# Moving the transposes of the left operand from the tensor engine to the vector engine in a matmul with layer norm

## Chip, cores, metric

One core of a Trainium2 chip. The metric is the device time of one execution in microseconds (us), median of several executions. All runs quoted are fast. A profiled execution has a span 1.8 to 2.1 us below the time measured for it.

## The reference

```python
def setup_inputs():
    m, k, n = 2048, 2048, 2048      # a, b, gamma, beta are fp32 normal draws; eps = 1e-5

def reference(a, b, gamma, beta, eps):
    x = np.matmul(a, b)
    mean = np.mean(x, axis=-1, keepdims=True)
    var = np.var(x, axis=-1, keepdims=True)
    normalized = (x - mean) / np.sqrt(var + eps)
    return (gamma * normalized + beta).astype(np.float32)
```

## The kernel before

All of `b` is loaded and cast to fp16 in SBUF. The rows of `a` are worked through in 16 blocks of 128 rows. The matmuls of this kernel take both operands with K on the partitions, but `a` is loaded with its rows there, so each block is transposed: 16 transposes of 128x128 on TensorE into PSUM, which ScalarE copies to SBUF. A block is then 64 matmuls (16 steps of K times 4 quarters of 512 columns). VectorE takes statistics from PSUM, ScalarE copies the product out of PSUM, and VectorE subtracts and scales in two steps a quarter. The first four blocks are done together, first their left half of the columns, then their right half, because `b` is still arriving.

```python
    a16p = ctx.enter_context(tc.tile_pool(name="a16p", bufs=4))
    # ... (cut)
    def emit_transposes_half(i, h):
        a16 = a16_lst[i]
        at = at_lst[i]
        t_ps = psum.tile([P, n_kt // 2, P], FP16, tag="tps", bufs=1,
                         name=f"tps{i}_{h}")
        for j in range(n_kt // 2):
            nc.tensor.transpose(t_ps[:, j, :], a16[:, ts(h * 8 + j, P)], ident)
        nc.scalar.copy(at[:, ds(h * 8, 8), :], t_ps)
    # ... (cut)
    def quarter_done(i, q):
        nc.vector.bn_stats(bnst_l[i][:, q, :], c_ps_l[i][q])
        x_sb = xpool.tile([P, NB], FP32, tag="x_sb", name=f"x_{i}_{q}")
        nc.scalar.copy(x_sb, c_ps_l[i][q])
    # ... (cut) the steady blocks:
            for kt in range(n_kt):
                for q in range(n_nb):
                    emit_mm(i, q, kt)
                if kt == 4 and i + 2 < n_mt:
                    alloc_at(i + 2)
                    emit_transposes_half(i + 2, 0)
                if kt == 9 and i + 2 < n_mt:
                    emit_transposes_half(i + 2, 1)
            for q in range(n_nb):
                quarter_done(i, q)
        emit_ln_stats(i)
        if i - n_start < n_start:
            emit_ln_stt(i - n_start)      # outputs of one of the first four blocks
        emit_ln_stt(i, split_out=(2 if not last else 4))
```

Of the kernel before, what the change touches and what calls it, by code (L numbers as in the profile page):

```python
# [16 lines left out]
def kernel(  # L17
# [12 lines left out]
    K2, N = b.shape  # L30
    assert K == K2
    assert M % P == 0 and K % P == 0 and N % 2048 == 0
# [5 lines left out]

    n_start = 4
    assert n_mt > n_start  # L40

    if isinstance(eps, bass.AP):
        eps_ap = eps
        eps_val = None
    else:
        eps_ap = None
        eps_val = float(eps)
# [4 lines left out]
    atp = ctx.enter_context(tc.tile_pool(name="atp", bufs=6))  # L52
    xpool = ctx.enter_context(tc.tile_pool(name="xpool", bufs=20))
    upool = ctx.enter_context(tc.tile_pool(name="upool", bufs=4))
    cpool = ctx.enter_context(tc.tile_pool(name="cpool", bufs=2))
    stat = ctx.enter_context(tc.tile_pool(name="stat", bufs=4))
# [5 lines left out]
    ident = konst.tile([P, P], FP16)  # L62

    b16 = bpool.tile([P, n_kt, N], FP16)

    def emit_a_load(i, split=1):
        a16 = a16p.tile([P, K], FP16, tag="a16", name=f"a16_{i}")
        w = K // split
        for s in range(split):
            nc.gpsimd.dma_start(a16[:, ds(s * w, w)], a[ts(i, P), ds(s * w, w)])  # L70
        return a16

    a16_lst = [None] * (n_mt + 2)
    at_lst = [None] * (n_mt + 1)

    def alloc_at(i):
        at_lst[i] = atp.tile([P, n_kt, P], FP16, tag="at", name=f"at{i}")

    def emit_transposes_half(i, h):
        a16 = a16_lst[i]  # L80
        at = at_lst[i]
        t_ps = psum.tile([P, n_kt // 2, P], FP16, tag="tps", bufs=1,
                         name=f"tps{i}_{h}")
        for j in range(n_kt // 2):
            nc.tensor.transpose(t_ps[:, j, :], a16[:, ts(h * 8 + j, P)], ident)  # L85
        nc.scalar.copy(at[:, ds(h * 8, 8), :], t_ps)  # L86

    def emit_transposes(i):
        alloc_at(i)
        emit_transposes_half(i, 0)  # L90
        emit_transposes_half(i, 1)
        return at_lst[i]

    bnst_l = [None] * n_mt
    c_ps_l = [[None] * n_nb for _ in range(n_mt)]
    x_sb_l = [[None] * n_nb for _ in range(n_mt)]
    rstd_l = [None] * n_mt
    mv_l = [None] * n_mt

    def alloc_q(i, q):  # L100
        if bnst_l[i] is None:
            bnst_l[i] = stat.tile([P, n_nb, 6], FP32, tag="bnst", name=f"bnst{i}")
        c_ps_l[i][q] = psum.tile([P, NB], FP32, tag="c_ps", bufs=7,
                                 name=f"cps_{i}_{q}")

    def emit_mm(i, q, kt):
        nc.tensor.matmul(  # L107
            c_ps_l[i][q],
            at_lst[i][:, kt, :],
            b16[:, kt, ds(q * NB, NB)],  # L110
            start=(kt == 0),
            stop=(kt == n_kt - 1),
        )

    def quarter_done(i, q):
        nc.vector.bn_stats(bnst_l[i][:, q, :], c_ps_l[i][q])  # L116
        x_sb = xpool.tile([P, NB], FP32, tag="x_sb", name=f"x_{i}_{q}")
        nc.scalar.copy(x_sb, c_ps_l[i][q])  # L118
        x_sb_l[i][q] = x_sb

    def emit_ln_stats(i):
        mv = stat.tile([P, 2], FP32, name=f"mv{i}")
        nc.vector.bn_aggr(mv, bnst_l[i])  # L123
        ve = stat.tile([P, 1], FP32, name=f"ve{i}")
        nc.vector.tensor_tensor(ve, mv[:, 1:2], eps_t, AluOp.add)  # L125
        sq = stat.tile([P, 1], FP32, name=f"sq{i}")
        nc.scalar.activation(sq, ve, ActFn.Sqrt)  # L127
        rstd = stat.tile([P, 1], FP32, name=f"rstd{i}")
        nc.vector.reciprocal(rstd, sq)  # L129
        mv_l[i] = mv  # L130
# [45 lines left out]
    for i in range(6, n_mt):  # L176
        a16_lst[i] = emit_a_load(i)
# [97 lines left out]
```

## Time and profile before

| | before |
|---|---|
| time, median of 15 runs | 268.2 us |
| TensorE: from first product matmul to last | 11.3 to 256.9 us |
| one steady block of 128 rows | 14.81 us, of it 13.8 matmuls and 0.9 transposes |
| VectorE busy in such a block | 13.6 us in the first four, 8.3 later |
| tail after the last matmul | 10.6 us |

The table is to be read from TensorE's side: it never waits between 29 us and the end, so the span is a start, then 13.8 + 0.9 us for each block, then a tail.

### The profile page before, as it was taken

Reading aid. Unit: us, or ns where it says so; the run is one execution under the profiler, and the core shown is the slowest. Engines: PE = TensorE matmul, PEld = TensorE weight load, DVE = VectorE, ACT = ScalarE, POOL = GpSimd, SP = SyncE. Lnnn points to the kernel's source line nnn. Section 1 sums busy time; section 2 is a strip of 40 time slices with the busy share of each in tenths; the row PEclk is TensorE's granted clock in tenths of the full one; section 3 lists DMA queues with packets and bytes.
Section 4 is the critical chain, followed back from the end, with each engine's and each line's share of the span. In section 5 each row is a group of like instructions: output and inputs, shape, how many; then the busy total and the mean of one; then the engine's idle time right before and its main releaser. Section 6 shows DMA issues by size and latency. Waiting matters only on the chain.

```text
span 267.5 us, 3149 instructions
## 1 busy us (share of the span) xinstructions
PE 242.8 (91%) x1280; PEld 117.0 (44%) x1280; DVE 131.9 (49%) x242; ACT 74.1 (28%) x114; POOL 30.3 (11%) x61
## 2 busy tenths in 40 slices
PE   1349999999999999999999999999999999999940
PEld 0125544454444445454444444454544444444410
DVE  0000000600059179898989183654729092847753
ACT  1314300750046133313315142323123151303110
POOL 8343433440000000000000000000000000000000
PEclk9999999999999999999999999999999999999995
DMA  5999999999930524937475515330211103030304
GB/s 74 164 209 210 210 213 208 210 210 370 214 70 0 176 59 161 219 160 156 175 152 211 159 29 167 71 157 0 117 42 80 78 29 130 0 157 2 157 0 157
DMA packets 12974, 35.85 MB, mean 134 GB/s; under 512 B 1440, under 2 KB 1952, under 8 KB 12704
## 3 DMA queue, kind: packets, MB, share of 16 engines
q0 software_dynamic: 8064, 18.88, 37.3%
q1 hardware_dynamic: 4896, 16.78, 15.7%
q8 instruction: 10, 0.16, 0.3%
q14 instruction: 4, 0.03, 0.0%
HBM read 35.65 MB, written 16.78 MB: 196 GB/s over the span
## 4 chain that ended last, share of the span: by engine, by line
PE 89%; DMA 4%; POOL 2%; DVE 2%; issue 0%; DVEq 0%; POOLq 0%
PE cps L107 84%; PE tps L85 5%; DMA b<-in_b_dram 4%; POOL a L70 2%; DVE u L140 1%; DVE c L144 1%; DVE bnst L116 0%; DVEq L270 0%; POOL b L164 0%; POOL b L153 0%; POOL ident L155 0%; DVE mv L123 0%; DVE ve L125 0%; DVE rstd L129 0%; POOLq L155 0%
## 5 line engine op out<-in xcount | busy, mean ns | idle before, releaser
L107 PE MATMUL cps<-b,at 128*128 128x512 f16 x1024 | 230.3, 382 | 7.1 <-DMA b<-in_b_dram 7.1
L107 PEld LDWEIGHTS <-at 128*128 128x128 f16 x1024 | 99.5, 98 | 122.7 <-issue 11.5
L116 DVE BATCH_NORM_STATS2 bnst<-cps 128x6 f32<-128x512 f32 x64 | 40.0, 685 | 129.6 <-PE cps L107 129.6
L118 ACT COPY x<-cps 128x512 f32<-128x512 f32 x64 | 37.4, 586 | 99.9 <-DVE bnst L116 99.1
L86 ACT COPY at<-tps 128x1024 f16<-128x1024 f16 x32 | 32.4, 1012 | 83.0 <-PE tps L85 83.0
L140 DVE SCALAR_TENSOR_TENSOR u<-x,mv,gamma_b 128x512 f32<-128x512 f32 x64 | 45.9, 743 | 0.0
L144 DVE SCALAR_TENSOR_TENSOR c<-u,rstd,beta_b 128x512 f32<-128x512 f32 x64 | 45.1, 744 | 0.0
L85 PE MATMUL tps<-ident,a 128*128 128x128 f16 x256 | 22.4, 233 | 7.0 <-DMA a<-in_a_dram 5.8
L85 PEld LDWEIGHTS <-a 128*128 128x128 f16 x256 | 18.9, 105 | 16.6 <-DMA a<-in_a_dram 6.4
L70 POOL DMA_DIRECT2D a<-in_a_dram x22 | 11.9, 546 | 110.0 <-PE tps L85 102.7
L173 POOL DMA_DIRECT2D b<-in_b_dram x16 | 8.5, 530 | 13.7 <-DMA b<-in_b_dram 9.9
L169 POOL DMA_DIRECT2D b<-in_b_dram x13 | 6.9, 530 | 9.7 <-DMA b<-in_b_dram 5.0
L123 DVE BATCH_NORM_AGGREGATE mv<-bnst 128x2 f32<-128x24 f32 x16 | 3.9, 254 | 0.4
L127 ACT ACTIVATE sq<-ve 128x1 f32<-128x1 f32 x16 | 3.1, 203 | 0.6 <-DVE ve L125 0.6
L125 DVE TENSOR_TENSOR ve<-mv,eps_t 128x1 f32<-128x1 f32 x16 | 2.3, 154 | 0.4
L129 DVE RECIPROCAL rstd<-sq 128x1 f32<-128x1 f32 x16 | 2.4, 157 | 0.3 <-ACT sq L127 0.3
L86 ACT ACT_TABLE_LOAD x1 | 1.3, 1283 | 0.7 <-PEq L256 0.7
L127 ACT ACT_TABLE_LOAD x1 | 1.3, 1283 | 0.0
L174 POOL DMA_DIRECT2D gamma_b<-in_gamma_dram x1 | 0.5, 530 | 0.8 <-DMA b<-in_b_dram 0.8
L175 POOL DMA_DIRECT2D beta_b<-in_beta_dram x1 | 0.5, 530 | 0.7 <-DMA b<-in_b_dram 0.7
L164 POOL DMA_DIRECT2D b<-in_b_dram x1 | 0.6, 577 | 0.0
L153 POOL DMA_DIRECT2D b<-in_b_dram x1 | 0.6, 565 | 0.0
(8 smaller groups left out, 1.4 us busy)
## 6 DMA issues: line engine op xcount, KB each, us to landing
out_dram<-c SPq DMA_DIRECT2D x30, 512.0 KB, 2.6
b<-in_b_dram POOLq DMA_DIRECT2D x32, 256.0 KB, 9.7
a<-in_a_dram POOLq DMA_DIRECT2D x12, 512.0 KB, 8.9
a<-in_a_dram POOLq DMA_DIRECT2D x6, 256.0 KB, 10.4
gamma_b<-in_gamma_dram POOLq DMA_DIRECT2D x1, 1024.0 KB, 11.0
beta_b<-in_beta_dram POOLq DMA_DIRECT2D x1, 1024.0 KB, 12.2
out_dram<-c SPq DMA_DIRECT2D x4, 256.0 KB, 2.6
a<-in_a_dram POOLq DMA_DIRECT2D x4, 128.0 KB, 4.5
```

The lines of the kernel that those rows point to most:

```text
L70: nc.gpsimd.dma_start(a16[:, ds(s * w, w)], a[ts(i, P), ds(s * w, w)])
L85: nc.tensor.transpose(t_ps[:, j, :], a16[:, ts(h * 8 + j, P)], ident)
L86: nc.scalar.copy(at[:, ds(h * 8, 8), :], t_ps)
L107: nc.tensor.matmul(c_ps_l[i][q], at_lst[i][:, kt, :], b16[:, kt, ds(q * NB, NB)], start=(kt == 0), stop=(kt == n_kt - 1),)
L116: nc.vector.bn_stats(bnst_l[i][:, q, :], c_ps_l[i][q])
L118: nc.scalar.copy(x_sb, c_ps_l[i][q])
L123: nc.vector.bn_aggr(mv, bnst_l[i])
L127: nc.scalar.activation(sq, ve, ActFn.Sqrt)
L140: nc.vector.scalar_tensor_tensor(u, x_sb_l[i][q], mv[:, 0:1], gamma_b[:, qs], AluOp.subtract, AluOp.mult,)
L144: nc.vector.scalar_tensor_tensor(c_sb[:, qs], u, rstd, beta_b[:, qs], AluOp.mult, AluOp.add,)
L169: nc.gpsimd.dma_start(b16[:, kt, 0:NH], b[ts(kt, P), 0:NH])
L173: nc.gpsimd.dma_start(b16[:, kt, NH:N], b[ts(kt, P), NH:N])
```

## The change

The intent: TensorE should do matmuls alone. The program uses VectorE's transpose within squares of 32x32, and the loads place the data such that this suffices. A block of `a` is loaded as four pieces: partition quadrant q (32 partitions) gets quarter q of K, and the four groups of 32 rows lie side by side. After transposing every 32x32 square, the 128 partitions hold 128 different values of K and the free dimension the 128 rows. K is thereby permuted (partition p at step t holds K = 16p + t), and `b` is loaded with its rows in the same order. Further parts:

- From the fifth block on, ScalarE first copies the block so that the squares are contiguous; the first four blocks are transposed straight from what was loaded, with a step of 16 elements.
- The product of these later blocks stays in PSUM (8 buffers of 128x512 fp32; the kernel before had 7 and one for the transposes) until VectorE's output steps read it; ScalarE's copy out of PSUM goes.
- The outputs of the first four blocks are spread in halves over the steady blocks 4 to 11.
- Within a steady block TensorE finishes one quarter after the other (`q` is now the outer loop, the step of K the inner), so that VectorE's statistics come one by one and not four at the end.
- 30 matmuls on zeros run at the start, the order of instructions on each engine is fixed by the program, and the small addition of eps moves into the square root.

```diff
-        for j in range(n_kt // 2):
-            nc.tensor.transpose(t_ps[:, j, :], a16[:, ts(h * 8 + j, P)], ident)
-        nc.scalar.copy(at[:, ds(h * 8, 8), :], t_ps)
... (cut)
+    b_rows = b.rearrange("(p t) n -> t p n", t=16)
+    a_first = a.rearrange("(s r) (q k) -> q r s k", r=32, q=4)
... (cut)
+    def load_a(i):
+        a_in[i] = a16p.tile([P, 4, KQ], FP16, tag="a16", name=f"a{i}")
+        for q in range(4):
+            nc.gpsimd.dma_start(
+                a_in[i][ds(32 * q, 32)], a_first[q][:, ds(4 * i, 4), :])
... (cut)
+    def permute(i):
+        p_in[i] = permp.tile([P, 4, KQ], FP16, tag="perm", name=f"perm{i}")
+        nc.scalar.copy(
+            p_in[i].rearrange("p j (b r) -> p j b r", r=32),
+            a_in[i].rearrange("p j (r b) -> p j b r", r=32),
+        )
+
+    def transpose_part(i, h):
+        if i >= G:
+            nc.vector.transpose(
+                at[i][:, ds(8 * h, 8), :].rearrange("p b (j r) -> p j b r", r=32),
+                p_in[i][:, :, ds(256 * h, 256)].rearrange("p j (b r) -> p j b r", r=32),
+            )
+            return
+        nc.vector.transpose(
+            at[i][:, ds(8 * h, 8), :].rearrange("p b (j r) -> p j b r", r=32),
+            a_in[i].rearrange("p j (r b) -> p j b r", r=32)[:, :, ds(8 * h, 8), :],
+        )
... (cut)
+        for _ in range(30):
+            nc.tensor.matmul(w_ps, warm[:, 0:P], warm, start=True, stop=True)
+
+        for g in range(G):
+            load_a(g)
+            for t in (2 * g, 2 * g + 1):
+                load_b(t, 0, NH)
... (cut)
+            if i > G:
+                normalise(i - 1)
             for q in range(n_nb):
... (cut)
+                bank(i, q)
+                for t in range(n_kt):
+                    mm(i, q, t)
+                if q == 0 and not last:
+                    permute(i + 1)
+                stats(i, q)
+                if q == 1 and not last:
+                    new_at(i + 1)
+                    transpose_part(i + 1, 0)
+                if q == 2 and not last:
+                    transpose_part(i + 1, 1)
+                if q == 3 and i < 3 * G:
+                    normalise((i - G) // 2, (i - G) % 2)
```

More of the change, by code (lines that the diff above doesn't have):

```diff
@@ L29 @@
     M, K = a.shape
-    K2, N = b.shape
-    assert K == K2
-    assert M % P == 0 and K % P == 0 and N % 2048 == 0
+    _, N = b.shape
     n_mt = M // P
@@ L37 @@
     NH = N // 2
-    n_start = 4
-    assert n_mt > n_start
-    if isinstance(eps, bass.AP):
-        eps_ap = eps
-        eps_val = None
-    else:
-        eps_ap = None
-        eps_val = float(eps)
+    G = 4
+    KQ = K // 4
     konst = ctx.enter_context(tc.tile_pool(name="konst", bufs=1))
@@ L51 @@
     a16p = ctx.enter_context(tc.tile_pool(name="a16p", bufs=4))
-    atp = ctx.enter_context(tc.tile_pool(name="atp", bufs=6))
-    xpool = ctx.enter_context(tc.tile_pool(name="xpool", bufs=20))
+    atp = ctx.enter_context(tc.tile_pool(name="atp", bufs=7))
+    first = ctx.enter_context(tc.tile_pool(name="first", bufs=1))
+    xpool = ctx.enter_context(tc.tile_pool(name="xpool", bufs=16))
     upool = ctx.enter_context(tc.tile_pool(name="upool", bufs=4))
     cpool = ctx.enter_context(tc.tile_pool(name="cpool", bufs=2))
-    stat = ctx.enter_context(tc.tile_pool(name="stat", bufs=4))
+    stat = ctx.enter_context(tc.tile_pool(name="stat", bufs=6))
     psum = ctx.enter_context(tc.tile_pool(name="psum", bufs=1, space=bass.MemoryType.PSUM))
@@ L61 @@
     eps_t = konst.tile([P, 1], FP32)
-    ident = konst.tile([P, P], FP16)
+    warm = konst.tile([P, NB], FP16)
     b16 = bpool.tile([P, n_kt, N], FP16)
-    def emit_a_load(i, split=1):
-        a16 = a16p.tile([P, K], FP16, tag="a16", name=f"a16_{i}")
-        w = K // split
-        for s in range(split):
-            nc.gpsimd.dma_start(a16[:, ds(s * w, w)], a[ts(i, P), ds(s * w, w)])
-        return a16
-    a16_lst = [None] * (n_mt + 2)
-    at_lst = [None] * (n_mt + 1)
-    def alloc_at(i):
-        at_lst[i] = atp.tile([P, n_kt, P], FP16, tag="at", name=f"at{i}")
@@ L79, in emit_transposes_half @@
-    def emit_transposes_half(i, h):
-        a16 = a16_lst[i]
-        at = at_lst[i]
-        t_ps = psum.tile([P, n_kt // 2, P], FP16, tag="tps", bufs=1,
-                         name=f"tps{i}_{h}")
-        for j in range(n_kt // 2):
-            nc.tensor.transpose(t_ps[:, j, :], a16[:, ts(h * 8 + j, P)], ident)
-        nc.scalar.copy(at[:, ds(h * 8, 8), :], t_ps)
-    def emit_transposes(i):
-        alloc_at(i)
-        emit_transposes_half(i, 0)
-        emit_transposes_half(i, 1)
-        return at_lst[i]
@@ L94 @@
-    bnst_l = [None] * n_mt
-    c_ps_l = [[None] * n_nb for _ in range(n_mt)]
-    x_sb_l = [[None] * n_nb for _ in range(n_mt)]
-    rstd_l = [None] * n_mt
-    mv_l = [None] * n_mt
-    def alloc_q(i, q):
-        if bnst_l[i] is None:
-            bnst_l[i] = stat.tile([P, n_nb, 6], FP32, tag="bnst", name=f"bnst{i}")
-        c_ps_l[i][q] = psum.tile([P, NB], FP32, tag="c_ps", bufs=7,
-                                 name=f"cps_{i}_{q}")
-    def emit_mm(i, q, kt):
-        nc.tensor.matmul(
-            c_ps_l[i][q],
-            at_lst[i][:, kt, :],
-            b16[:, kt, ds(q * NB, NB)],
-            start=(kt == 0),
-            stop=(kt == n_kt - 1),
-        )
@@ L115, in quarter_done @@
-    def quarter_done(i, q):
-        nc.vector.bn_stats(bnst_l[i][:, q, :], c_ps_l[i][q])
-        x_sb = xpool.tile([P, NB], FP32, tag="x_sb", name=f"x_{i}_{q}")
-        nc.scalar.copy(x_sb, c_ps_l[i][q])
-        x_sb_l[i][q] = x_sb
-    def emit_ln_stats(i):
+    b_rows = b.rearrange("(p t) n -> t p n", t=16)
+    a_cols = a.rearrange("(t j r) (q k) -> t j q r k", j=4, r=32, q=4)
+    a_first = a.rearrange("(s r) (q k) -> q r s k", r=32, q=4)
+    permp = ctx.enter_context(tc.tile_pool(name="permp", bufs=2))
@@ new lines, with load_b, load_a_first, transpose_first @@
+    p_in = {}
+    bnst, x_of, mv_of, rs_of, at, a_in, c_of = {}, {}, {}, {}, {}, {}, {}
+    def load_b(t, lo, w):
+        nc.gpsimd.dma_start(b16[:, t, ds(lo, w)], b_rows[t][:, ds(lo, w)])
+    def load_a_first():
+        w = KQ // 4
+        f = first.tile([P, G * 4, w], FP32, name="a_first32")
+        for q in range(4):
+            nc.sync.dma_start(
+                f[ds(32 * q, 32)], a_first[q][:, 0 : 4 * G, ds(0, w)])
+        a_in["g", 0] = f
+    def transpose_first(g):
+        w = first.tile([P, 4, P], FP32, name=f"at32_{g}")
+        nc.vector.transpose(
+            w.rearrange("p b (j r) -> p j b r", r=32),
+            a_in["g", 0][:, ds(4 * g, 4), :].rearrange("p j (b r) -> p j b r", r=32),
+        )
+        nc.scalar.copy(at[g][:, 0:4, :], w)
@@ new lines, in load_a_group @@
+    def load_a_group(c):
+        w = KQ // 4
+        a_in["g", c] = a16p.tile([P, G * 4, w], FP16, tag="a16", name=f"ag{c}")
+        for q in range(4):
+            nc.gpsimd.dma_start(
+                a_in["g", c][ds(32 * q, 32)],
+                a_first[q][:, 0 : 4 * G, ds(c * w, w)],
+            )
+    def load_a(i):
+        a_in[i] = a16p.tile([P, 4, KQ], FP16, tag="a16", name=f"a{i}")
+        for q in range(4):
+            nc.gpsimd.dma_start(
+                a_in[i][ds(32 * q, 32)], a_first[q][:, ds(4 * i, 4), :])
@@ new lines, in new_at, with transpose_group @@
+    def new_at(i):
+        at[i] = atp.tile([P, n_kt, P], FP16, tag="at", name=f"at{i}")
+    def transpose_group(c, g):
+        nc.vector.transpose(
+            at[g][:, ds(4 * c, 4), :].rearrange("p b (j r) -> p j b r", r=32),
+            a_in["g", c][:, ds(4 * g, 4), :].rearrange("p j (b r) -> p j b r", r=32),
+        )
[4 more added lines that the diff above has]
+            a_in[i].rearrange("p j (r b) -> p j b r", r=32),
+        )
@@ new lines, in transpose_part @@
+    def transpose_part(i, h):
+        if i >= G:
+            nc.vector.transpose(
+                at[i][:, ds(8 * h, 8), :].rearrange("p b (j r) -> p j b r", r=32),
+                p_in[i][:, :, ds(256 * h, 256)].rearrange("p j (b r) -> p j b r", r=32),
+            )
+            return
+        nc.vector.transpose(
+            at[i][:, ds(8 * h, 8), :].rearrange("p b (j r) -> p j b r", r=32),
+            a_in[i].rearrange("p j (r b) -> p j b r", r=32)[:, :, ds(8 * h, 8), :],
+        )
@@ new lines, in bank, with mm, stats, evacuate @@
+    def bank(i, q):
+        x_of[i, q] = psum.tile([P, NB], FP32, tag="c_ps", bufs=8, name=f"ps_{i}_{q}")
+    def mm(i, q, kt):
+        nc.tensor.matmul(
+            x_of[i, q], at[i][:, kt, :], b16[:, kt, ds(q * NB, NB)],
+            start=(kt == 0), stop=(kt == n_kt - 1),
+        )
+    def stats(i, q):
+        if i not in bnst:
+            bnst[i] = stat.tile([P, n_nb, 6], FP32, tag="bnst", name=f"bnst{i}")
+        nc.vector.bn_stats(bnst[i][:, q, :], x_of[i, q])
+    def evacuate(i, q):
+        x = xpool.tile([P, NB], FP32, tag="x_sb", name=f"x_{i}_{q}")
+        nc.scalar.copy(x, x_of[i, q])
+        x_of[i, q] = x
@@ L122, in emit_ln_stats, with aggregate @@
+    def aggregate(i):
         mv = stat.tile([P, 2], FP32, name=f"mv{i}")
-        nc.vector.bn_aggr(mv, bnst_l[i])
-        ve = stat.tile([P, 1], FP32, name=f"ve{i}")
-        nc.vector.tensor_tensor(ve, mv[:, 1:2], eps_t, AluOp.add)
+        nc.vector.bn_aggr(mv, bnst[i])
         sq = stat.tile([P, 1], FP32, name=f"sq{i}")
-        nc.scalar.activation(sq, ve, ActFn.Sqrt)
-        rstd = stat.tile([P, 1], FP32, name=f"rstd{i}")
-        nc.vector.reciprocal(rstd, sq)
-        mv_l[i] = mv
@@ L131, in emit_ln_stats @@
-        rstd_l[i] = rstd
-    def emit_ln_stt(i, split_out=2):
-        mv, rstd = mv_l[i], rstd_l[i]
-        c_sb = cpool.tile([P, N], FP32, tag="c_sb", name=f"c{i}")
-        nq_per_out = n_nb // split_out
-        for q in range(n_nb):
-            qs = ds(q * NB, NB)
-            u = upool.tile([P, NB], FP32, tag="u", name=f"u_{i}_{q}")
-            nc.vector.scalar_tensor_tensor(
-                u, x_sb_l[i][q], mv[:, 0:1], gamma_b[:, qs],
-                AluOp.subtract, AluOp.mult,
-            )
-            nc.vector.scalar_tensor_tensor(
-                c_sb[:, qs], u, rstd, beta_b[:, qs],
-                AluOp.mult, AluOp.add,
-            )
-            if (q + 1) % nq_per_out == 0:
-                o = ds((q + 1 - nq_per_out) * NB, nq_per_out * NB)
-                nc.sync.dma_start(out[ts(i, P), o], c_sb[:, o])
@@ L152 @@
-    a16_lst[0] = emit_a_load(0, split=4)
-    nc.gpsimd.dma_start(b16[:, 0, 0:NH], b[ts(0, P), 0:NH])
-    nc.vector.memset(ident, 0.0)
-    nc.gpsimd.affine_select(
-        out=ident, in_=ident, compare_op=AluOp.not_equal, fill=1.0,
-        base=0, pattern=[[-1, P]], channel_multiplier=1,
-    )
-    if eps_ap is not None:
-        nc.sync.dma_start(eps_t, eps_ap.unsqueeze(0).to_broadcast([P, 1]))
-    else:
-        nc.vector.memset(eps_t, eps_val)
-    a16_lst[1] = emit_a_load(1, split=2)
@@ L164 @@
-    nc.gpsimd.dma_start(b16[:, 1, 0:NH], b[ts(1, P), 0:NH])
-    a16_lst[2] = emit_a_load(2, split=2)
-    nc.gpsimd.dma_start(b16[:, 2, 0:NH], b[ts(2, P), 0:NH])
-    a16_lst[3] = emit_a_load(3, split=2)
-    for kt in range(3, n_kt):
-        nc.gpsimd.dma_start(b16[:, kt, 0:NH], b[ts(kt, P), 0:NH])
-    a16_lst[4] = emit_a_load(4)
-    a16_lst[5] = emit_a_load(5)
-    for kt in range(n_kt):
-        nc.gpsimd.dma_start(b16[:, kt, NH:N], b[ts(kt, P), NH:N])
-    nc.gpsimd.dma_start(gamma_b, gamma.unsqueeze(0).to_broadcast([P, N]))
@@ L175 @@
-    nc.gpsimd.dma_start(beta_b, beta.unsqueeze(0).to_broadcast([P, N]))
-    for i in range(6, n_mt):
-        a16_lst[i] = emit_a_load(i)
-    startup_pairs_L = [(p, q) for p in range(n_start) for q in (0, 1)]
-    startup_pairs_R = [(p, q) for p in range(n_start) for q in (2, 3)]
-    for (p, q) in startup_pairs_L:
-        alloc_q(p, q)
-    for i in range(n_start):
-        alloc_at(i)
-    emit_transposes_half(0, 0)
-    emit_transposes_half(0, 1)
-    for q in (0, 1):
-        emit_mm(0, q, 0)
@@ L189 @@
-    for p in range(1, n_start):
-        emit_transposes_half(p, 0)
-        emit_transposes_half(p, 1)
-        for pp in range(p):
-            for q in (0, 1):
-                emit_mm(pp, q, p)
-        for kt in range(p + 1):
-            for q in (0, 1):
-                emit_mm(p, q, kt)
-    for kt in range(n_start, n_kt):
-        for (p, q) in startup_pairs_L:
-            emit_mm(p, q, kt)
-    for (p, q) in startup_pairs_L:
-        quarter_done(p, q)
-    for (p, q) in startup_pairs_R:
-        alloc_q(p, q)
@@ L205 @@
-    for kt in range(n_kt):
-        for (p, q) in startup_pairs_R:
-            emit_mm(p, q, kt)
-        if kt == 0:
-            at_lst[4] = emit_transposes(4)
-        if kt == 2:
-            at_lst[5] = emit_transposes(5)
-    for (p, q) in startup_pairs_R:
-        quarter_done(p, q)
-    for p in range(n_start):
-        emit_ln_stats(p)
-    for i in range(n_start, n_mt):
-        last = i == n_mt - 1
-        for q in range(n_nb):
-            alloc_q(i, q)
-        if last:
-            for q in range(n_nb):
-                for kt in range(n_kt):
-                    emit_mm(i, q, kt)
-                quarter_done(i, q)
-        else:
-            for kt in range(n_kt):
-                for q in range(n_nb):
-                    emit_mm(i, q, kt)
-                if kt == 4 and i + 2 < n_mt:
-                    alloc_at(i + 2)
-                    emit_transposes_half(i + 2, 0)
-                if kt == 9 and i + 2 < n_mt:
-                    emit_transposes_half(i + 2, 1)
-            for q in range(n_nb):
-                quarter_done(i, q)
-        emit_ln_stats(i)
-        if i - n_start < n_start:
-            emit_ln_stt(i - n_start)
-        emit_ln_stt(i, split_out=(2 if not last else 4))
@@ new lines, in aggregate, with invert, centre, scale @@
+        nc.scalar.activation(sq, mv[:, 1:2], ActFn.Sqrt, bias=eps_t)
+        mv_of[i] = mv
+        return sq
+    def invert(i, sq):
+        rs = stat.tile([P, 1], FP32, name=f"rs{i}")
+        nc.vector.reciprocal(rs, sq)
+        rs_of[i] = rs
+    def centre(i, q, u):
+        nc.vector.scalar_tensor_tensor(
+            u, x_of[i, q], mv_of[i][:, 0:1], gamma_b[:, ds(q * NB, NB)],
+            AluOp.subtract, AluOp.mult,
+        )
+    def scale(i, q, u, c):
+        nc.vector.scalar_tensor_tensor(
+            c[:, ds(q * NB, NB)], u, rs_of[i], beta_b[:, ds(q * NB, NB)],
+            AluOp.mult, AluOp.add,
+        )
@@ new lines, in normalise @@
+    def normalise(i, h=None):
+        if h in (None, 0):
+            sq = aggregate(i)
+            c_of[i] = cpool.tile([P, N], FP32, tag="c_sb", name=f"c{i}")
+        c = c_of[i]
+        for half in (0, 1) if h is None else (h,):
+            us = []
+            for q in (2 * half, 2 * half + 1):
+                us.append(upool.tile([P, NB], FP32, tag="u", name=f"u_{i}_{q}"))
+                centre(i, q, us[-1])
+                if q == 0:
+                    invert(i, sq)
+            for q in (2 * half, 2 * half + 1):
+                scale(i, q, us[q % 2], c)
+            o = ds(half * NH, NH)
+            nc.sync.dma_start(out[ts(i, P), o], c[:, o])
@@ new lines, in normalise_last @@
+    def normalise_last(i):
+        sq = aggregate(i)
+        c = cpool.tile([P, N], FP32, tag="c_sb", name=f"c{i}")
+        centre(i, 0, x_of[i, 0])
+        invert(i, sq)
+        for q in range(4):
+            if q:
+                centre(i, q, x_of[i, q])
+            scale(i, q, x_of[i, q], c)
+            o = ds(q * NB, NB)
+            nc.sync.dma_start(out[ts(i, P), o], c[:, o])
+    order = {
+        mybir.EngineType.PE, mybir.EngineType.DVE, mybir.EngineType.Activation,
+        mybir.EngineType.Pool, mybir.EngineType.SP,
+    }
@@ new lines @@
+    with tc.manual_schedule(engines=order):
+        nc.vector.memset(warm, 0.0)
+        nc.vector.memset(eps_t, float(eps))
+        w_ps = psum.tile([P, NB], FP32, tag="c_ps", bufs=8, name="w_ps")
+        for _ in range(30):
[4 more added lines that the diff above has]
+                load_b(t, 0, NH)
+        for t in range(8, n_kt):
+            load_b(t, 0, NH)
+        for t in range(8):
+            load_b(t, NH, NH)
+        load_a(4)
+        for t in range(8, n_kt):
+            load_b(t, NH, NH)
+        nc.gpsimd.dma_start(gamma_b, gamma.unsqueeze(0).to_broadcast([P, N]))
+        nc.gpsimd.dma_start(beta_b, beta.unsqueeze(0).to_broadcast([P, N]))
+        for i in range(5, n_mt):
+            load_a(i)
+        for g in range(G):
+            new_at(g)
+            for q in (0, 1):
+                bank(g, q)
+        for g in range(G):
+            for h in (0, 1):
+                transpose_part(g, h)
+        for p in range(G):
+            for t in range(2 * p):
+                for q in (0, 1):
+                    mm(p, q, t)
+            for t in (2 * p, 2 * p + 1):
+                for g in range(p + 1):
+                    for q in (0, 1):
+                        mm(g, q, t)
+        for t in range(8, 12):
+            for g in range(G):
+                for q in (0, 1):
+                    mm(g, q, t)
+        for g in range(G):
+            for q in (0, 1):
+                for t in range(12, n_kt):
+                    mm(g, q, t)
+                stats(g, q)
+                evacuate(g, q)
+        for g in range(G):
+            for q in (2, 3):
+                bank(g, q)
+        for t in range(12):
+            for g in range(G):
+                for q in (2, 3):
+                    mm(g, q, t)
+        new_at(4)
+        permute(4)
+        for h in (0, 1):
+            transpose_part(4, h)
+        for g in range(G):
+            for q in (2, 3):
+                for t in range(12, n_kt):
+                    mm(g, q, t)
+                stats(g, q)
+                evacuate(g, q)
+        for i in range(G, n_mt):
+            last = i == n_mt - 1
+            if i > G:
+                normalise(i - 1)
+            for q in range(n_nb):
+                bank(i, q)
[11 more added lines that the diff above has]
+                    normalise((i - G) // 2, (i - G) % 2)
+        normalise_last(n_mt - 1)
```

## The prediction

> **What bounds the kernel now.** I read the page first: busy time, slices, chain of waits, groups of instructions.
>
> ```profile
> PE 242.8 (91%) x1280; PEld 117.0 (44%) x1280; DVE 131.9 (49%) x242; ACT 74.1 (28%) x114; POOL 30.3 (11%) x61
> PE   1349999999999999999999999999999999999940
> DVE  0000000600059179898989183654729092847753
> DMA  5999999999930524937475515330211103030304
> ...
> PE cps L107 84%; PE tps L85 5%; DMA b<-in_b_dram 4%; POOL a L70 2%; DVE u L140 1%; DVE c L144 1%; DVE bnst L116 0%; DVEq L270 0%; POOL b L164 0%; POOL b L153 0%; POOL ident L155 0%; DVE mv L123 0%; DVE ve L125 0%; DVE rstd L129 0%; POOLq L155 0%
> ...
> L116 DVE BATCH_NORM_STATS2 bnst<-cps 128x6 f32<-128x512 f32 x64 | 40.0, 685 | 129.6 <-PE cps L107 129.6
> L86 ACT COPY at<-tps 128x1024 f16<-128x1024 f16 x32 | 32.4, 1012 | 83.0 <-PE tps L85 83.0
> L140 DVE SCALAR_TENSOR_TENSOR u<-x,mv,gamma_b 128x512 f32<-128x512 f32 x64 | 45.9, 743 | 0.0
> L85 PE MATMUL tps<-ident,a 128*128 128x128 f16 x256 | 22.4, 233 | 7.0 <-DMA a<-in_a_dram 5.8
> ```
>
> TensorE is full from the fourth slice (20 us) nearly to the end; the others wait for it. The chain is 84% product matmuls (L107) and 5% transposes of `a` (L85), with a start led by loads and a short VectorE tail. So the cost of an item on TensorE is time, and VectorE has room, though in slices 17 to 22 it is already at 80 to 90%.
>
> Second, the timeline of TensorE over one steady block of 128 rows:
>
> ```profile
> 100.63 4.48 PE L107 MATMUL cps<-b,at 128*128 128x512 f16 x20
> 104.94 0.61 PE L85 MATMUL tps<-ident,a 128*128 128x128 f16 x8
> 105.39 9.77 PE L107 MATMUL cps<-b,at 128*128 128x512 f16 x44
> 115.00 0.61 PE L85 MATMUL tps<-ident,a 128*128 128x128 f16 x8
> 115.44 4.48 PE L107 MATMUL cps<-b,at 128*128 128x512 f16 x20
> ```
>
> Take starts, since durations overlap: 20 matmuls in 4.31 us, 0.216 each; 8 transposes in 0.45 us, 0.056 each. A block is 64 x 0.216 + 16 x 0.056 = 14.7, measured 14.81 (100.63 to 115.44). All 1024 matmuls are 221.2 us, all 256 transposes 14.3. The last matmul ends at 256.9, so 256.9 - 221.2 - 14.3 = 21.4 us is TensorE's start: waiting, and running at half rate.
>
> Third, the timeline of the start, for when loads land:
>
> ```profile
> 15.35 1.01 PE L107 MATMUL cps<-b,at 128*128 128x512 f16 x2 [3.04 <-DMA b<-in_b_dram]
> 19.11 1.01 PE L107 MATMUL cps<-b,at 128*128 128x512 f16 x2 [1.89 <-DMA b<-in_b_dram]
> 20.77 2.34 PE L107 MATMUL cps<-b,at 128*128 128x512 f16 x5
> 26.89 0.61 PE L85 MATMUL tps<-ident,a 128*128 128x128 f16 x8
> ```
>
> The first line waits for the second row of `b` (1.5 MiB issued up to there, counted as written in fp16), the next for the third (2.25 MiB): 5.0 us per MiB, the page's 210 GB/s. A transfer with C MiB issued up to its end thus lands at 7.9 + 5.0 C.
>
> Fourth, VectorE at the end:
>
> ```profile
> 257.62 0.26 DVE L123 BATCH_NORM_AGGREGATE mv<-bnst 128x2 f32<-128x24 f32 x1
> 258.00 0.75 DVE L140 SCALAR_TENSOR_TENSOR u<-x,mv,gamma_b 128x512 f32<-128x512 f32 x1
> 259.38 1.41 DVE L144 SCALAR_TENSOR_TENSOR c<-u,rstd,beta_b 128x512 f32<-128x512 f32 x2
> 260.71 1.41 DVE L140 SCALAR_TENSOR_TENSOR u<-x,mv,gamma_b 128x512 f32<-128x512 f32 x2
> 262.04 1.41 DVE L144 SCALAR_TENSOR_TENSOR c<-u,rstd,beta_b 128x512 f32<-128x512 f32 x2
> ```
>
> A pair of normalising steps starts every 1.33 us, so one takes 0.66 us of VectorE in a run, not its 743 ns. The tail from last matmul to the end of the span is 10.6 us.
>
> [...] at 20.8 us the matmuls start 0.43 us apart, from 25.6 on 0.216.
>
> **The change part by part.** Removed: all TensorE transposes, 14.3 us on the path, and ScalarE's 32 copies behind them, which are off it. *Start.* Before every matmul there are 30 on zeros, on an otherwise idle engine: they cost nothing[...]. The loads now go a0, b0, b1, a1, b2, b3, a2, b4, b5, a3 (each a is 0.5 MiB in four transfers, each half row of b 0.25), so a3 is complete at C = 3.5: 25.4 us. Its packets are 1 KB; single DMA packets in the trace take a median 98 ns for 1 KB against 173 for 2 KB, 13% more per byte, so 2 MiB of a add 1.3: 26.7. Its first half is transposed at 28.5. By the static order, matmuls of the fourth row block begin only then, with 28 + 32 + 32 = 92 left in the left half: 19.9 us, to 48.4; the rows of b that they need land earlier (C = 6, 38 us). The right half is 128 x 0.216 = 27.6: 76.0. *Steady.* Twelve blocks of 64 x 0.216 = 13.82, 13.85 with gaps: 166.2, to 242.2. The start is then 242.2 - 221.2 = 21.0 us against 21.4: unchanged, and what is gained is the 14.3 of transposes, 14.7 in all. *VectorE* gets two transposes a block and the first four blocks' outputs in halves over eight blocks. A loaded block there is 4 statistics x 0.62 + [...]12 x 0.66 + [...]0.6 small = 13.6 us, against TensorE's 13.85: it just fits. Within the block, counted from its first matmul: last statistics of the block before 0.7, half an old output 3.1, the whole previous output 6.2 (10.0), two statistics (11.2), transpose (12.4), statistics (13.0), transpose (14.2). TensorE wants the first half at 13.85 and the second eight matmuls later, 15.6: 1.4 us to spare. I add 0.5 us for stalls. *PSUM* now serves to the output steps, freed before TensorE returns to a bank. *Tail.* The last block's steps go subtract, scale, subtract, scale, each on the one just before, so nearly 0.75 each in place of 0.66, less one small add: +0.8 us.
>
> Sum: 268.5 - 14.7 + 0.5 + 0.8 = 255.1; I say 255.
>
> **The rivals.** *VectorE becomes the bound.* For it: 13.6 of 13.85 us leaves nothing. With transposes of 1.5 us a block is 14.3, 0.45 over in eight blocks less 1.4 to spare: 2.2 in all, about 257. [...] I give 20% to more than 1 us[...]. *The start gets worse.* For it: small transfers to 32 partitions, four issues of some 0.55 us a block, [...]half rate for the 20 matmuls of the third block costs 4 us, some of it hidden by the wait for a3. Against: the load engines were already over 90% busy there. 2 to 6 us: 257 to 261. *The start gets better.* If a0 to a3 land sooner, or both halves are as cheap as 1.2 us, TensorE could start 2 to 5 us earlier: 249 to 253. The limit is the loads: nothing beats some 35 us for the left half's 6 MiB. *The transposes were hidden anyway*, as in a kernel bound by loads: the steady blocks of 14.8 us, with 13.8 of matmuls and no waits, speak against it.
>
> **Range and chances.** The 14.3 us rest on a pitch read directly; the start is uncertain by some 4 us either way, VectorE by 0 to 8 upwards. I take 248 to 262. Below 263.1 counts as faster by over 2%[...]: faster 0.90, same 0.08, slower 0.02.
>
> **What would show it.** Right: no transposes on TensorE; steady blocks 13.8 to 13.9 us; VectorE transposes near 1.2 us, some 1.8 at the start; VectorE about 95% busy in the middle third and below 80% at the end; last matmul near 242 to 243; tail near 11.4. Wrong: steady blocks of 14.5 us or more, with TensorE waiting for VectorE's transposes; left half ending after 53 us; or subtract steps from PSUM well above 0.8 us.

From the sum of VectorE's loaded block two terms are cut, the two transposes and an addition for the subtract steps that read PSUM: with them it came to 13.6 us, and what is left adds up to 11.0. The 1.2 us (contiguous) and 1.8 us (step of 16 elements) that the prediction goes on to use were guesses, as its trace has no such instruction; in the changed kernel they took 1.22 and 2.00 us. Three remarks on TensorE's pace are cut: what sets it, that it falls in waits, and that matmuls on zeros may help; the 0.43 and 0.216 us between starts are measured, their cause is not. The forecast's own sum, 255.1 us, has lost no term. The 35 us for the left half is an estimate; in that trace the first landing is at 5.0 us, and 6 MiB at 5.0 us each are 30 more.

## The result

| | before | after |
|---|---|---|
| time, median | 268.22 us (267.86 to 269.25, 15 runs) | 253.15 us (252.34 to 254.27, 11 runs) |
| ratio | | 0.944 (0.942 to 0.945) |

A ratio is the mean time of one kernel's fast runs over that of the other's of the same rounds, so not quite the ratio of the medians.

The page of the changed kernel: busy time, slices, chain, then groups (line, engine, operation, operands, shapes and count; busy us, mean ns of one; idle time before and what ended it).

```profile
PE 233.5 (93%) x1054; PEld 103.9 (41%) x1054; DVE 175.6 (70%) x258; ACT 62.6 (25%) x46; POOL 53.5 (21%) x102
DVE  0477602621072579998999899998999895968463
...
L109 ACT COPY perm<-a 128x2048 f16<-128x2048 f16 x12 | 47.0, 3918 | 1.7 <-DMA a<-in_a_dram 1.7
...
L116 DVE STREAM_TRANSPOSE at<-perm 128x1024 f16<-128x1024 f16 x24 | 29.3, 1224 | 6.2 <-ACT perm L109 6.2
L159 DVE SCALAR_TENSOR_TENSOR u<-ps,mv,gamma_b 128x512 f32<-128x512 f32 x44 | 31.6, 743 | 0.4
L121 DVE STREAM_TRANSPOSE at<-a 128x1024 f16<-128x1024 f16 x8 | 15.7, 2000 | 13.1 <-DMA a<-in_a_dram 13.1
```

TensorE's transposes are gone and VectorE's busy time has risen from 131.9 to 175.6 us, with the middle of the span at 80 to over 90%. A transpose takes 1.22 us from contiguous squares and 2.00 us with the step of 16 elements. ScalarE's copy of 2048 elements, which reads with that step, takes 3.92 us; a contiguous copy of 1024 takes 1.04 us in b_no_tr, below. The subtract step reads PSUM in the same 743 ns in which it read SBUF before (741 ns from SBUF in this kernel).

The timeline of TensorE, whole (start, us, engine, line, operation, count, idle before and releaser):

```profile
1.19 8.65 PE L208 MATMUL w_ps<-warm 128*128 128x512 f16 x30 [1.19 <-DVE eps_t L205]
12.09 1.89 PE L130 MATMUL ps<-b,at 128*128 128x512 f16 x4 [2.25 <-DVE at L121]
17.85 4.97 PE L130 MATMUL ps<-b,at 128*128 128x512 f16 x12 [3.87 <-DVE at L121]
23.25 4.49 PE L130 MATMUL ps<-b,at 128*128 128x512 f16 x20 [0.44 <-DVE at L121]
28.12 213.47 PE L130 MATMUL ps<-b,at 128*128 128x512 f16 x988 [0.37 <-DVE at L121]
```

From 28.12 on, the chain of waits has one piece for everything up to the tail:

```profile
26.04 2.03 DVE at L121
...
28.12 213.49 PE ps L130 x988
```

So TensorE waits in the start for the transposes of each of the first four blocks (the 4, 12, 20 and 988 matmuls each begin with one), and after 28.12 us for nothing: 213.49 us over 988 matmuls is 0.216 us each, the pitch of the kernel before, without a gap. The steady blocks are 13.82 us.

VectorE in one loaded steady block (timeline of VectorE, from the last statistics of one block to those of the next):

```profile
103.50 0.70 DVE L138 BATCH_NORM_STATS2 bnst<-ps 128x6 f32<-128x512 f32 x1 [0.40 <-PE ps L130]
104.11 1.40 DVE L159 SCALAR_TENSOR_TENSOR u<-x,mv,gamma_b 128x512 f32<-128x512 f32 x2
...
107.04 0.75 DVE L159 SCALAR_TENSOR_TENSOR u<-ps,mv,gamma_b 128x512 f32<-128x512 f32 x1
...
113.60 1.23 DVE L116 STREAM_TRANSPOSE at<-perm 128x1024 f16<-128x1024 f16 x1
...
115.34 1.22 DVE L116 STREAM_TRANSPOSE at<-perm 128x1024 f16<-128x1024 f16 x1
117.31 0.70 DVE L138 BATCH_NORM_STATS2 bnst<-ps 128x6 f32<-128x512 f32 x1 [0.76 <-PE ps L130]
```

Between 103.50 and 117.31 lie 13.81 us, one block of TensorE, and VectorE idles for 0.76 of them (0.40 in the block before, which has a few small steps more). It needs 13.0 to 13.4 us of 13.8. Its second transpose ends at 116.56, before the next block begins at about 117.2.

### The profile page after: what moved, and what is told of

Read it like the earlier page. It is cut to its first block, busy times and chain, and to the rows that moved or that the text cites. A ratio compares the mean times of both kernels' runs of the same rounds, so it can differ in the third digit from the quotient of the medians.

```text
span 252.4 us, 2680 instructions
## 1 busy us (share of the span) xinstructions
PE 233.5 (93%) x1054; PEld 103.9 (41%) x1054; DVE 175.6 (70%) x258; ACT 62.6 (25%) x46; POOL 53.5 (21%) x102
## 4 chain that ended last, share of the span: by engine, by line
PE 85%; DMA 8%; DVE 3%; POOL 1%; issue 1%; DVEq 0%; POOLq 0%
PE ps L130 85%; DMA a<-in_a_dram 5%; DMA b<-in_b_dram 3%; DVE c L165 1%; DVE ps L159 1%; POOL a L95 1%; DVE at L121 1%; DVE bnst L138 0%; POOL b L65 0%; DVE mv L147 0%; DVE rs L155 0%; DVEq L121 0%; POOLq L303 0%
## 5 line engine op out<-in xcount | busy, mean ns | idle before, releaser
L130 PE MATMUL ps<-b,at 128*128 128x512 f16 x1024 | 224.8, 383 | 6.9 <-DVE at L121 6.9
L138 DVE BATCH_NORM_STATS2 bnst<-ps 128x6 f32<-128x512 f32 x64 | 43.2, 690 | 51.9 <-PE ps L130 51.9
L95 POOL DMA_DIRECT2D a<-in_a_dram x64 | 34.8, 548 | 98.5 <-ACT perm L109 80.8
L109 ACT COPY perm<-a 128x2048 f16<-128x2048 f16 x12 | 47.0, 3918 | 1.7 <-DMA a<-in_a_dram 1.7
L165 DVE SCALAR_TENSOR_TENSOR c<-u,rs,beta_b 128x512 f32<-128x512 f32 x60 | 42.2, 745 | 0.0
L116 DVE STREAM_TRANSPOSE at<-perm 128x1024 f16<-128x1024 f16 x24 | 29.3, 1224 | 6.2 <-ACT perm L109 6.2
L159 DVE SCALAR_TENSOR_TENSOR u<-ps,mv,gamma_b 128x512 f32<-128x512 f32 x44 | 31.6, 743 | 0.4
L121 DVE STREAM_TRANSPOSE at<-a 128x1024 f16<-128x1024 f16 x8 | 15.7, 2000 | 13.1 <-DMA a<-in_a_dram 13.1
L142 ACT COPY x<-ps 128x512 f32<-128x512 f32 x16 | 9.4, 586 | 60.2 <-DVE bnst L138 60.2
L65 POOL DMA_DIRECT2D b<-in_b_dram x32 | 17.5, 546 | 15.2 <-DMA b<-in_b_dram 11.2
L159 DVE SCALAR_TENSOR_TENSOR u<-x,mv,gamma_b 128x512 f32<-128x512 f32 x16 | 11.5, 741 | 0.1
```

Source lines behind the costliest of these rows:

```text
L65: nc.gpsimd.dma_start(b16[:, t, ds(lo, w)], b_rows[t][:, ds(lo, w)])
L95: nc.gpsimd.dma_start(a_in[i][ds(32 * q, 32)], a_first[q][:, ds(4 * i, 4), :])
L109: nc.scalar.copy(p_in[i].rearrange("p j (b r) -> p j b r", r=32), a_in[i].rearrange("p j (r b) -> p j b r", r=32),)
L116: nc.vector.transpose(at[i][:, ds(8 * h, 8), :].rearrange("p b (j r) -> p j b r", r=32), p_in[i][:, :, ds(256 * h, 256)].rearrange("p j (b ...
L121: nc.vector.transpose(at[i][:, ds(8 * h, 8), :].rearrange("p b (j r) -> p j b r", r=32), a_in[i].rearrange("p j (r b) -> p j b r", r=32)[: ...
L130: nc.tensor.matmul(x_of[i, q], at[i][:, kt, :], b16[:, kt, ds(q * NB, NB)], start=(kt == 0), stop=(kt == n_kt - 1),)
```

## The experiments

The theory: the gain is the TensorE time of the removed transposes, VectorE takes them over with little to spare, and the start is about what it was. The rivals: the gain comes from the start (order of loads, matmuls on zeros); or VectorE is not near its limit at all.

### b_no_tr: the kernel before, without transposes on TensorE

```diff
-        t_ps = psum.tile([P, n_kt // 2, P], FP16, tag="tps", bufs=1, ...)
-        for j in range(n_kt // 2):
-            nc.tensor.transpose(t_ps[:, j, :], a16[:, ts(h * 8 + j, P)], ident)
-        nc.scalar.copy(at[:, ds(h * 8, 8), :], t_ps)
+        nc.scalar.copy(at[:, ds(h * 8, 8), :],
+                       a16[:, ds(h * 8 * P, 8 * P)].rearrange("p (j c) -> p j c", c=P))
```

> The kernel before without its TensorE transposes: ScalarE copies the loaded rows straight to where the transposed ones went (wrong result on purpose; same 32 copies, loads and matmuls). Theory (the gain is the transposes' TensorE time, 256 x 0.056 = 14.3 us, on the path): about 253.5 us, 251 to 256, steady blocks of 13.8 us. Rival (the gain comes from the start, that is from the order of the loads and the matmuls on zeros, and the transposes were hidden): 264 us or more.

Measured: 256.6 us (ratio to before 0.958, 0.951 to 0.965). That is far from the rival's 264 and 0.6 above the range I gave. TensorE's timeline shows why:

```profile
44.61 29.53 PE L104 MATMUL cps<-b,at 128*128 128x512 f16 x128 [2.46 <-ACT x L115]
74.73 170.21 PE L104 MATMUL cps<-b,at 128*128 128x512 f16 x784 [0.58 <-ACT x L115]
```

TensorE waited 3.0 us for ScalarE's evacuation of banks. The scheduler had put the copies of the fifth and sixth block, which wait for late loads, ahead of these evacuations. This is a wait that my edit made.

### b_no_tr2: the same, with ScalarE in program order

```diff
+    with tc.manual_schedule(engines={mybir.EngineType.Activation}):
         ... (everything from the first product matmul on, indented)
```

> As b_no_tr (the kernel before without its TensorE transposes, wrong result on purpose), with ScalarE's instructions held in program order. In b_no_tr the scheduler had put the copies of the fifth and sixth block in front of the evacuations of the left half, and TensorE waited 2.5 us and 0.6 us for these. Theory (these waits are an artefact of the experiment, the rest is the transposes): 2 to 3 us less than b_no_tr's 256.6, so 253.5 to 254.7, no wait over 1 us after the left half. Rival (the 14.3 us were not all on the path, and 256.6 is what the removal alone is worth): still 256 or more.

Measured: 254.1 us (0.947, 0.943 to 0.951), and TensorE now runs from 18.9 us to its end with no wait that the timeline sets apart:

```profile
18.87 223.50 PE L104 MATMUL cps<-b,at 128*128 128x512 f16 x1016 [1.40 <-DMA b<-in_b_dram]
```

Taking the transposes off TensorE is thus worth 268.3 - 254.1 = 14.2 us, with an uncertainty of about 1; the prediction's figure was 14.3. The edit also fixes the order of ScalarE and lets it copy from SBUF and not from PSUM. These alone can hardly have gained anything, since TensorE waits for nothing after 29 us in the kernel before. Only 192 of the transposes lie in the steady blocks; the first sixteen of the other 64 ended at 9.1 us, while TensorE was still waiting for `b` (11.3 us), so the last 3 to 4 us of the 14.2 belong to the start as a whole. What the rest of the change adds is not resolved (254.1 against 253.2, with intervals that overlap), and may be a sum of gains and losses.

### a_dummy_tr: as many small matmuls put back

```diff
                 bank(i, q)
+                for _ in range(4):
+                    nc.tensor.matmul(x_of[i, q][:, 0:P], warm[:, 0:P], warm[:, 0:P],
+                                     start=True, stop=True)
                 for t in range(n_kt):
```

> The changed kernel with 16 matmuls of 128 columns on zeros put back into each of the 12 steady row blocks, 192 of them, each into the bank that the next matmul clears. Theory: 192 x 0.056 = 10.8 us more than the changed kernel, about 264 us, steady blocks 14.7 us, VectorE with more idle time. Rival (start): below 255.

Measured: 264.5 us, 11.2 above the changed kernel where 10.8 were expected. A block is now 14.70 us (75.39 to 90.09):

```profile
75.39 0.39 PE L276 MATMUL ps<-warm 128*128 128x128 f16 x4
...
90.09 0.39 PE L276 MATMUL ps<-warm 128*128 128x128 f16 x4
```

The rival that the start makes the gain is out for these 11 us of the 15: the same start with the TensorE time put back gives the time back.

### a_strided: VectorE's transposes made dearer

```diff
-        if i >= G:
+        if False:
             nc.vector.transpose(
... (cut; both calls of permute are removed as well)
```

> The changed kernel with ScalarE's permuting copy left out: VectorE transposes all row blocks with the step of 16 elements, as it does for the first four (2.00 us each in place of 1.22; correct result). Theory (VectorE has 0.4 to 0.8 us idle in a loaded block of 13.8 us): 1.6 us more in each of seven loaded blocks, 1.0 us over each, less the margin of about 1 us: 6 us more, about 259 us, loaded blocks of 14.7 to 15 us, light ones 13.8. Rival (VectorE has room enough, only TensorE sets the time): within 1 us of the changed kernel's 253.

Measured: 259.3 us (0.968), 6.1 above. TensorE's timeline:

```profile
118.46 14.25 PE L130 MATMUL ps<-b,at 128*128 128x512 f16 x64 [0.27 <-DVE at L121]
133.31 13.99 PE L130 MATMUL ps<-b,at 128*128 128x512 f16 x64 [0.60 <-DVE at L121]
147.82 14.26 PE L130 MATMUL ps<-b,at 128*128 128x512 f16 x64 [0.52 <-DVE at L121]
```

From start to start the blocks are 14.85 and 14.51 us, and every one begins with a wait for VectorE's transposes. A full VectorE block sets the pace here. So the ScalarE copy, which costs 3.9 us a block on an engine that is busy for 25% of the span, buys 6 us, and the margin of VectorE in the changed kernel is real but small.

### a_whole_old: the outputs of the first four blocks not spread

```diff
-                if q == 3 and i < 3 * G:
-                    normalise((i - G) // 2, (i - G) % 2)
+                if q == 3 and i < 2 * G:
+                    normalise(i - G)
```

> The changed kernel with the outputs of the first four row blocks not spread in halves over eight blocks but written whole in the first four steady ones, as the kernel before did (correct result). Theory: VectorE needs 16.0 us in four windows of 13.8, 2.2 over each, 9 in all less a margin of 2.4: about 6.6 us more, 260 us; TensorE waits for transposes in blocks 6 to 9. Rival (room enough): within 1 us of 253.

Measured: 261.7 us (0.977), 8.4 above. TensorE's timeline:

```profile
105.13 13.99 PE L130 MATMUL ps<-b,at 128*128 128x512 f16 x64 [0.62 <-DVE at L116]
121.08 15.67 PE L130 MATMUL ps<-b,at 128*128 128x512 f16 x64 [1.96 <-DVE at L116]
137.02 13.99 PE L130 MATMUL ps<-b,at 128*128 128x512 f16 x64 [0.27 <-DVE at L116]
152.97 96.87 PE L130 MATMUL ps<-b,at 128*128 128x512 f16 x448 [1.96 <-DVE at L116]
```

The first wait is 0.62, and the three blocks between these starts are 15.95 us each, 2.13 over 13.82: 7.0 us in all, near the 6.6 expected. The two profiled executions are 8.2 us apart (262.5 and 254.3); the rest is the start, in which this one began its long run of matmuls at 29.2 us and not at 28.1. Spreading the outputs was thus a necessary part of the change, not tidying. That VectorE has room enough is refuted twice.

### The start: a_again, a_no_warm, a_quarters, a_wide_loads

These ran on one chip in five rounds, with the changed kernel as control.

> The changed kernel once more, as the control on the chip of this group: 253 us, 252 to 254.5.

Measured: 253.2 us (253.1 to 253.3). The outputs are right.

```diff
-        for _ in range(30):
+        for _ in range(1):
             nc.tensor.matmul(w_ps, warm[:, 0:P], warm, start=True, stop=True)
```

> The changed kernel with 1 matmul on zeros at the start in place of 30. Theory (the start is set by the landing of the fourth block of a and its transpose; the trace shows 12 matmuls at half rate after 17.9 us in spite of them, and 0.4 us of waiting left before the fourth block): within 0.5 us of the control. Rival (they [...]pay for themselves): 2 to 4 us slower.

Measured: 253.4 us. The matmuls on zeros are worth nothing that these runs can resolve. In the changed kernel the 12 matmuls at 17.85 us still start 0.42 us apart, nearly twice 0.216, after a wait of 3.9 us. What sets this slower pitch is not shown. No fixed length of wait does in these runs: the four matmuls at 12.09 us start 0.42 us apart too after a wait of 2.25 us, while twelve in a_wide_loads (below) take 2.76 us together, 0.216 each from start to start, after 2.21. The profile's clock column does not always show it either: from 14 to 21 us it reads 0.50 in the changed kernel and 1.00 in a_no_warm, whose 12 matmuls are as slow (4.99 us). The pitch is the safer reading.

```diff
-            for h in (0, 1):
-                transpose_part(g, h)
+            for t0, n in ((0, 4), (4, 4), (8, 8)):
+                nc.vector.transpose(
... (cut; steps t0 to t0 + n of K of one of the first four blocks)
```

The second edit, to the last block's output steps, is left out here: centre, centre, scale, scale for each half in place of centre, scale for each quarter.

> The changed kernel with two small repairs (correct result): the first halves of the first four blocks' transposes cut in two, so that the first matmuls of a block wait 1.0 us and not 2.0 after the landing; and the last block's output steps in pairs (subtract, subtract, scale, scale) in place of one by one. Theory: 0.8 to 1.1 us less at the start, about 0.4 less in the tail (each step on the one just before starts 0.73 us after it, in pairs 0.66): 1.2 to 1.5 us under the control, 251.7. Rival (the start is bound by the rows of b, not by a3's transpose): only the 0.4 of the tail.

Measured: 252.2 us (0.942, 0.938 to 0.946), 1.1 under the control in the medians, but the intervals of the two ratios overlap. In its profile the last step of VectorE ends 6.5 us after the last matmul, against 7.0; the long run of matmuls began at 26.45 us, against 27.13 in the control's profile. Both are about as large as expected, though the start varies by as much between executions. It is correct and the fastest correct kernel here, by a margin too small to be sure of.

```diff
-        for q in range(4):
-            nc.gpsimd.dma_start(
-                a_in[i][ds(32 * q, 32)], a_first[q][:, ds(4 * i, 4), :])
+        nc.gpsimd.dma_start(a_in[i], a[ts(i, P), :].rearrange("p (j k) -> p j k", j=4))
```

> The changed kernel with each block of a loaded by one transfer to all 128 partitions, contiguous rows of 8 KB, in place of four transfers to 32 partitions in pieces of 2 KB (wrong result on purpose; same bytes). Theory (my sum put 1.3 us on the small packets, and the first block landed at 10.0 us, against 7.1 in the kernel before): the fourth block's transpose starts 1 to 2 us earlier, 251.5 to 252.5 us. Rival (the pieces cost nothing, the rate of the load engines alone counts): as the control, within 0.4 us.

Measured: 250.1 us (0.933, 0.930 to 0.937): 3.1 under the control, twice what I expected. The timeline of VectorE shows the fourth block's transposes starting at 21.2 us, against 25.1 in the control (the control's line first):

```profile
25.05 3.94 DVE L121 STREAM_TRANSPOSE at<-a 128x1024 f16<-128x1024 f16 x2 [1.16 <-DMA a<-in_a_dram]
21.20 3.93 DVE L119 STREAM_TRANSPOSE at<-a 128x1024 f16<-128x1024 f16 x2 [1.01 <-DMA a<-in_a_dram]
```

The stretches of 7 us show where (us; each engine's busy time and instructions; clock, DMA share, GB/s written), first the control, then this kernel:

```profile
7.00:14.00 7.00, 4.64 (x21) 1.88 (x19) 3.94 (x2) 0.00 (x0) 3.05 (x6) 1.00 1.06 153
14.00:21.00 7.00, 4.16 (x11) 1.54 (x12) 4.95 (x3) 0.00 (x0) 4.67 (x9) 0.51 1.17 206
```

```profile
7.00:14.00 7.00, 4.79 (x23) 1.98 (x22) 5.97 (x4) 0.00 (x0) 2.23 (x5) 1.00 1.11 213
14.00:21.00 7.00, 4.79 (x23) 2.03 (x22) 5.14 (x3) 0.00 (x0) 2.11 (x4) 1.00 1.08 211
```

With whole blocks the loads run at 213 and 211 GB/s from 7 us on; in pieces they reach 153 from 7 to 14 us and come near that rate only from 14 us (206 GB/s here, 197 in the profile of the result).

### Which property of the pieces costs: a_wide_four, a_wide_pieces, a_near_pieces

The changed kernel's loads differ from whole blocks in three ways: four times as many transfers, 32 partitions each, and pieces of 2 KB read and 1 KB written. These three runs were on two other chips, without a control of their own; they are compared by their ratios to the kernel before in the same rounds (control: 0.945, 0.942 to 0.948).

```diff
 a_wide_four:    four transfers, each to 128 partitions, one piece of 2 KB for each
+            nc.gpsimd.dma_start(a_in[i][:, q, :], a[ts(i, P), ds(q * KQ, KQ)])
 a_wide_pieces:  one transfer, four pieces for each partition, from rows 512 rows apart
+        rows = a.rearrange("(j p) (c k) -> c p j k", j=4, k=KQ)
+        nc.gpsimd.dma_start(a_in[i], rows[i % 4][ds(128 * (i // 4), 128)])
 a_near_pieces:  the same, from four neighbouring rows
+        rows = a.rearrange("(p j) (c k) -> c p j k", j=4, k=KQ)
+        nc.gpsimd.dma_start(a_in[i], rows[i % 4][ds(128 * (i // 4), 128)])
```

> The changed kernel with each block of a in four transfers, as it has, but each to all 128 partitions and one 2 KB piece (1 KB written) wide (wrong result on purpose; same bytes). a_wide_loads saved 3.1 us and the fourth block's transposes began at 21.2 us instead of 25 to 26. If what it saved is the number of transfers (8 may be in flight, so pieces of 128 KB hold less in flight, and each takes 0.55 us to issue) or the size of the piece: about 253 us, as the control. If it is the spread over 32 partitions: about 250.

Measured: 253.1 us (0.943, 0.941 to 0.945). The spread over 32 partitions costs nothing that these runs resolve. The 0.55 us is the 548 ns that GpSimd takes for an issue in the changed kernel's page; the eight in flight is what the landings in both kernels' traces give: at none of GpSimd's issues of loads (56 before, 98 after) were more than eight under way, the new one counted.

> The changed kernel with each block of a in one transfer to 128 partitions, but made of four pieces of 2 KB for each partition that are not neighbours in memory (wrong result on purpose; same bytes). If the size of the piece is what costs: about 253 us, or 1.3 us above a_wide_loads by my own packet figure, 251.4. If the number of transfers or the spread over 32 partitions costs: about 250.

Measured: 261.7 us (0.975), outside of all I had allowed for. The loads ran at 128 to 165 GB/s from 7 to 28 us. With its pieces 4 MB apart this run measures an access pattern, not a piece size, and says nothing on the question. Why that distance is slow I have not tested.

> As a_wide_pieces (each block of a in one transfer to 128 partitions, in pieces of 2 KB, wrong result on purpose), but the four pieces of a partition come from neighbouring rows, 8 KB apart, and not from rows 4 MB apart[...]. If the number of transfers is what costs in the changed kernel (16 transfers of 128 KB against 4 of 512 KB in the start): about 250 us, fourth block's transposes from 21 to 22 us. If the size of the piece costs: about 253, transposes from 25.

Measured: 252.0 us (0.9405, 0.9375 to 0.944), between the two answers; the fourth block's transposes start at 23.6 us. By the medians, one transfer in place of four saves 1.2 us, and whole rows in place of pieces 1.9 more. The second figure compares one pattern of pieces only, and the ratio's interval overlaps the control's and all but touches that of a_wide_loads (0.930 to 0.937), so the split is rough. That both play a part is likely and not shown. One way in which the number of transfers can matter is visible: in a_wide_loads GpSimd issues eight transfers by 5.6 us and then waits 1.0 us for the first block to land before the ninth. Eight in flight (above) of 128 KB hold fewer bytes than eight of 512 KB. No run varied that number, and that it is what costs is not shown.

## Why the prediction was right, step by step

The prediction was 255, the result 253.2, and it came about as the sum said.

- *14.3 us of transposes on the path*: right. Removing them alone gave 14.2 (b_no_tr2), putting the 192 of the steady blocks back cost 11.2 for 10.8 (a_dummy_tr).
- *VectorE just fits, 13.6 of 13.85 us*: right in kind, on the cautious side in size. It needs 13.0 to 13.4. I had added something to each subtract step that reads PSUM; the trace shows no difference, 743 ns against 741 from SBUF. The contiguous transpose was guessed at 1.2 us and took 1.22. The 0.5 us for stalls were not used.
- *The rival of a bound VectorE*: not what happened, but the arithmetic of an overfull block holds. Making the transposes dearer cost 6.1 us for 6 expected, not spreading the outputs 8.4 for 6.6.
- *The start*: the fourth block's matmuls were to begin at 28.5 us and began at 28.1 (27.1 in the control). That agreement hides two errors. My line for landings, 7.9 + 5.0 us per MiB, was fitted to the kernel before, whose own first loads are cut in pieces and run at 169 GB/s between 7 and 14 us; with whole blocks the fourth block lands at 21.2 us with 3.5 MiB issued, which would be an intercept of 3.7. The line was thus 4.2 us too late for loads without pieces (that its own pieces are the reason is likely, not tested), and the 1.3 us that I added for small packets too little: in pieces the fourth block came 3.9 us later in the control and 4.8 in the profile of the result, about 3 us in the time. That the two errors nearly cancelled is luck. The half transpose with a step of 16 elements was guessed at 1.8 us and took 2.0.
- *The matmuls on zeros cost nothing*: they cost nothing, and did nothing for the time (253.2 us with 30, 253.4 with one).
- *The tail, 0.8 us more*: VectorE's part grew from 6.6 to 7.0 us after the last matmul, the whole tail from 10.6 to 10.8. In the dependent sequence steps start 0.67 and 0.79 us after one another by turns, 0.73 in the mean, not 0.75.

The sum forecast a gain of 13.4 us (268.5 to 255.1); the two profiled executions are 15.0 apart and the medians 15.1. The difference is made of the last matmul, which ended at 241.6 us and not 242.2 (0.4 in the start, the rest in gaps that I had allowed between blocks and that are not there), the stalls (0.5) and the tail (0.6). Another 0.3 of the 2 us between forecast and result is the median of the kernel before, 268.2 and not 268.5.

## What to carry to other kernels

When one engine is full from start to end, price what it does besides its main work by the pitch at which it starts, and look for another engine that can take it; here 256 transposes of 0.056 us were worth 14 us although each was short. Then add up the new load of the other engine over one period, instruction by instruction by its pitch, and spread what can wait: a sum of 13.4 us in 13.8 was free, while some 14.6 or 16 in single periods cost the excess once the margin was used up. A rate or an offset fitted to the start of one kernel carries that kernel's own way of loading with it.
